# Second mixer of a two-layer decoder step: the first half of the output projection is written ahead of the delta stage, and the memory projections are handed over in steps between the delta heads

## The chip, the cores and the metric

The kernel runs on one core of a Trainium2 chip. The metric is the device time of one execution in microseconds (us), the median of three runs. The profile is one more execution, taken by the hardware profiler. TensorE (PE in the rows; PEld is its weight load), VectorE (DVE), ScalarE (ACT), GpSimd (POOL) and the DMA queue of SyncE (SP) each work through a queue of their own, and semaphores tie them together.

## What is computed

The reference runs a trunk of two layers over 512 prompt tokens and 8 x 8 sample tokens (576 columns in all, width 1024). Each layer is a feed-forward block, a token mixer, a cross attention over 256 memory tokens and a second feed-forward block. The change is in the mixer of the second layer. Cut to what matters:

```python
def odd_mixer(h, ...):
    p = h @ w_in                                  # one input projection for both groups
    # group C: retention, 4 heads -> y_c (512 columns)
    # group D: RWKV-7 delta rule, 8 heads of 64 -> y_d (512 columns)
    #   S_t = S_{t-1} diag(w_t) + (S_{t-1} a_t) b_t^T + v_t k_t^T ;  o_t = S_t r_t
    return concat([y_c, y_d]) @ w_out             # one output projection, 1024 x 1024

def mem_kv(mem, mem_g, w_kv):                     # needs nothing of x
    k, v = split(rmsnorm(mem, mem_g) @ w_kv, 2)   # 256 x 1024 @ 1024 x 2048
```

So the half of the output projection that reads y_c can run as soon as the retention heads are done, and the keys and values of the memory can be computed at any time before the cross attention of that layer.

## The kernel before

**Layout.** Activations lie transposed, 128 features on the partitions and the 576 tokens along the free side, in two halves of 288 tokens (`TH`). A dense product is made from three fp32r products (`wh` and `wl` are the high and low part of a weight; `mm3`, line 331): eight output chunks, each over k = 4 or 8 blocks of 128, times three, times two halves. One half of the output projection is thus 8 x 4 x 3 x 2 = 192 matmuls of 288 columns. Its weights come in four loads of 0.5 MB through `unit` (line 300 issues the load, 317 casts `wh` on ScalarE, 318 makes `wl` on VectorE), and `add_x` (1597) adds each chunk to the residual.

**Memory projections.** `wkv` (lines 1396 to 1435) is a generator. Its first two steps load the memory, transpose it (1405) and form high and low parts (1412, 1413) in four buffers of the tag `y`. Its eight further steps are one unit each: a load of 1 MB (300), two casts on ScalarE (307), two subtractions on VectorE (308), 48 matmuls of 256 columns (lines 1427, 1428, 1429 in equal number), two scaled copies (1431), and, at the start of the next step, a store (1435). All eight are 384 matmuls. `y` has six buffers; the four split retention outputs `ys` and the two prepared pairs of heads 2 and 3 hold all six until the first half of the output projection is done.

**Delta stage.** `delta(j)` handles two of the eight 64-wide heads at once, so there are four of them, j = 0 to 3, in two lanes (j % 2). Each has: score matmuls (1134), a block inverse that goes through DRAM and back (`blocks`, lines 1062 to 1076) with 15 steps of small VectorE work (1070, 1073), products that complete the inverse (`inverse`), the operands of the recurrence, and then the recurrence itself, eight chunks in order. A step of it is two matmuls on TensorE, two additions on VectorE (1193), two matmuls, and the state update on VectorE (1200). A tail handles the sample tokens. `decays(j)` prepares a head, `bonus(j)` and `delta_out(j)` finish it. Heads 2 and 3 use the slots of heads 0 and 1 again, so they begin when those are through. In program order: `delta(0)`, `delta(1)`, `decays(2)`, `decays(3)`, `bonus`, `delta_out(0)`, `delta_out(1)`, `delta(2)`, `delta(3)`, `delta_out(2)`, `delta_out(3)`, first half of the output projection, all of `wkv`, second half.

**Order.** The queues are not written out by hand here. A planner runs over the whole program before it goes to the chip and lays each engine's instructions in a fixed order: of those that its own simulated clock says are ready, the one written earlier in the program goes first, and a later one is pulled ahead where the engine would otherwise be free and a buffer is there. On the chip each queue is then worked through in that fixed order. So what stands last in the program text need not run last.

Of the kernel before, what the change touches and what calls it, by code (L numbers as in the profile page):

```python
# [140 lines left out]
class Net:  # L141
# [1131 lines left out]
    def odd_mixer(self, filler, nxt):  # L1273
        nc, a, o = self.nc, self.a, self.o
        self.tmp = 't'
        self.lane = 0
        self.norm_finish()
        xn = self.xn
        w_in, w_out = a['odd_w_in'][0], a['odd_w_out'][0]
        tabs = []  # L1280
        for n in range(2):
            self.lane = 1
            t = self.ct('g')
            nc.sync.dma_start(t, a['c_rope'][:, n * T:(n + 1) * T])
            nc.vector.tensor_mul(t, t, self.rstd)
            tabs.append(t)
        self.cosr, self.sinr = tabs
        col = lambda g, h: w_in[:, g * 512 + h * P:g * 512 + (h + 1) * P]
        ys = []
        raw, ds, yd = {}, {}, {}  # L1290
        self.slot = [{}, {}]

        def proj(h):
            uq, uk = self.unit(col(0, h), col(1, h))
            qk = self.pair()
            q = self.rope(self.mm3(uq, xn), qk[:, 0])
            k = self.rope(self.mm3(uk, xn), qk[:, 1])
            uv, ug = self.unit(col(2, h), col(3, h))
            vt = self.token_major(self.col_scale(self.mm3(uv, xn)), 'm')
            return q, k, vt, self.silu_twice(self.mm3(ug, xn))  # L1300

        def mix(h, q, k, vt, sg):
            ys.append(self.head_norm(self.retention(h, q, k, vt), self.vec('ret_gnorm', h), sg, True))

        def low_rank():
            self.sh = self.cp.tile([P, 126], F32, tag="edge", bufs=1, name="sh")
            self.lh = self.cp.tile([P, 8], F32, name="lh")
            nc.scalar.mul(self.lh[:, :4], self.vec('rwkv_w0', 0, 4), 0.5)
            nc.scalar.mul(self.lh[:, 4:], self.vec('rwkv_a0', 0, 4), 0.5)
            self.la = self.kp.tile([P, T], F32, tag="acc", bufs=1, name="la")  # L1310
            uw, = self.unit(w_in[:, 3584:3712])
            self.shift_mix(self.mm3(uw, xn), 12, self.la)
            nc.scalar.activation(self.la[:64], self.la[:64], AF.Tanh)

        def gate():
            ug, = self.unit(w_in[:, 3712:3840])
            self.sgd = self.shift_mix(self.mm3(ug, xn), 13, None)
            nc.scalar.activation(self.sgd, self.sgd, AF.Tanh, scale=0.5)
            nc.vector.tensor_scalar(self.sgd, self.sgd, 0.5, 0.5, ALU.mult, ALU.add)
            ps = self.psm()  # L1320
            nc.tensor.transpose(ps[:126, :P], self.sh, self.ident)
            sht = self.small(P, tag="tok", bufs=3)
            nc.scalar.copy(sht[:126], ps[:126, :P])
            nc.sync.dma_start(o['shift_p'][0, 0].rearrange("(c p) -> c p", p=P), sht[:14])
            nc.sync.dma_start(o['shift_s'][0].rearrange("b (c p) -> (b c) p", p=P), sht[14:126])

        def decay(j):
            self.slot[j] = {f't{i}': self.ct('t') for i in range(3)}
            self.slot[j].update({f'g{i}': self.ct('g') for i in range(2, 6)})
            ds[j] = self.decays(j, *raw[j])  # L1330
            self.slot[j].update(g0=raw[j][0], g1=raw[j][1])

        for h in range(2):
            self.lane = h
            mix(h, *proj(h))
        self.lane = 0
        low_rank()
        raw[0] = self.prep(0, w_in)
        decay(0)
        self.lane = 1  # L1340
        for h in (2, 3):
            mix(h, *proj(h))
        raw[1] = self.prep(1, w_in)
        self.lane = 0
        self.bonus(ds[0])
        self.lane = 1
        decay(1)
        self.lane = 0
        ys = [self.split(y) for y in ys]
        raw[2] = self.prep(2, w_in)  # L1350
        self.lane = 1
        self.bonus(ds[1])
        raw[3] = self.prep(3, w_in)
        self.lane = 0
        gate()
        for n in range(2):
            self.lane = n
            wide = [self.ct2(n) for _ in range(4)]
            self.slot[n].update({f'x{i}': wide[i // 2][:, i % 2] for i in range(8)})
            self.slot[n].update({f't{i}': self.ct('t') for i in range(3)})  # L1360
        for pair in ((0, 1), (2, 3)):
            for j in pair:
                self.lane = j % 2
                self.delta(j, ds[j])
            for j in pair if pair[0] == 0 else ():
                self.lane = j % 2
                ds[j + 2] = self.decays(j + 2, *raw[j + 2])
            for j in pair if pair[0] == 0 else ():
                self.lane = j % 2
                self.bonus(ds[j + 2])  # L1370
            for j in pair:
                self.lane = j % 2
                yd[j] = self.delta_out(j, ds[j])
        self.lane = 0
        self.out_proj(w_out[:512], ys, None)
        self.run(filler())
        self.out_proj(w_out[512:], [self.split(yd[j]) for j in range(4)], nxt)


# [510 lines left out]
```

## Time and profile before

| | |
|---|---|
| median of 3 runs | 2960.69 us (2960.6 to 2961.26) |
| profiled execution | 2950.59 us |
| its span, first to last instruction | 2948.8 us |
| mean granted TensorE clock | 0.979 |
| TensorE busy (its ends are modelled) | 2872.8 us, 97% |
| VectorE / ScalarE / GpSimd busy | 2100.4 / 1253.9 / 421.7 us |

[...] Rows below are stamped in us from the start of the span.

### The profile page before, as it was taken

To read this page: it belongs to the slowest core of one execution; us is meant where nothing else is said; L and a number is where in the kernel's file an instruction comes from. 1 tells how busy PE (TensorE), PEld (TensorE's weight loads), DVE (VectorE), ACT (ScalarE), POOL (GpSimd) and SP (SyncE) were. 2 spreads that over 40 slices of the span, in tenths; PEclk is the share of its full clock that TensorE was granted. 3 is DMA by queue.
4 is the path that set the end of the run, shared out by engine and by line. 5 is a ranking of instruction groups with operands and counts; after the bars stand their busy time and mean duration, and the time that the engine had idled before them with its cause. 6 is when DMAs were issued, how large, how long until landed. Compare 5 with 4: busy or idle time off the path is not lost.

```text
span 2948.8 us, 54661 instructions
## 1 busy us (share of the span) xinstructions
PE 2872.8 (97%) x22324; PEld 2718.9 (92%) x22324; DVE 2100.4 (71%) x3786; ACT 1253.9 (43%) x2257; POOL 421.7 (14%) x384
## 2 busy tenths in 40 slices
PE   8999999999999999999999999999989999999998
PEld 8999998999988999999999999888768787999998
DVE  7988866555546698886988875657577546698884
ACT  6544442222535544445444444343243434544443
POOL 1100012111100210002100111213222100210001
PEclk9999999999999999999999999999779999999999
DMA  4332222222445232222323232222112235232322
GB/s 139 102 99 90 87 83 59 87 74 94 143 172 176 76 104 86 90 87 76 97 91 98 89 95 78 75 76 64 38 44 83 91 138 196 74 103 87 100 76 65
DMA packets 343250, 278.76 MB, mean 95 GB/s; under 512 B 27332, under 2 KB 326168, under 8 KB 343000
## 3 DMA queue, kind: packets, MB, share of 16 engines
q1 hardware_dynamic: 343000, 275.27, 29.6%
q8 instruction: 176, 2.88, 0.4%
q14 instruction: 74, 0.61, 0.1%
HBM read 262.09 MB, written 13.14 MB: 93 GB/s over the span
## 4 chain that ended last, share of the span: by engine, by line
PE 86%; DVE 6%; ACT 3%; DMA 2%; issue 2%; POOL 1%; SPq 0%; ACTq 0%; POOLq 0%; DVEq 0%
PE pm L347 23%; PE pd L331 21%; PE pd L1768 18%; PE pd L347 4%; PE pd L1741 3%; PE pm L1741 2%; PE pm L1025 2%; PE pm L945 1%; DVE wf L1648 1%; PE pd L1459 1%; DMA S<-ffn_w_down 1%; PE pd L1428 1%; PE pm L509 1%; PE pd L1427 1%; PE pd L1429 1%
## 5 line engine op out<-in xcount | busy, mean ns | idle before, releaser
L347 PE MATMUL pm<-xf,wf 128*128 128x288 f32 x5472 | 763.7, 295 | 1.8 <-DVE g L566 1.6
L347 PEld LDWEIGHTS pm<-xf,wf 128*128 128x128 f32 x5472 | 740.6, 188 | 2.6 <-ACT wf L1647 1.8
L331 PE MATMUL pd<-x,wh 128*128 128x288 f32 x2368 | 430.8, 301 | 1.2 <-ACT t L894 1.2
L331 PEld LDWEIGHTS pd<-x,wh 128*128 128x128 f32 x2368 | 354.7, 191 | 6.5 <-ACT t L894 1.4
L1597 DVE SCALAR_TENSOR_TENSOR xT<-pd,xT 128x576 f32<-128x576 f32 x240 | 181.3, 756 | 249.0 <-PE pd L1768 185.5
L1768 PE MATMUL pd<-m,wf 128*128 128x288 f32 x2112 | 339.0, 296 | 5.5 <-DVE xT L1597 3.5
L1768 PE MATMUL pd<-g,wf 128*128 128x288 f32 x2112 | 337.9, 295 | 0.0
L560 POOL TENSOR_TENSOR g<-g,rstd 128x576 f32<-128x576 f32 x88 | 152.2, 1746 | 1271.9 <-DVE t L1680 561.9
L1768 PEld LDWEIGHTS pd<-m,wf 128*128 128x128 f32 x2112 | 301.1, 188 | 7.5 <-issue 4.4
L1768 PEld LDWEIGHTS pd<-g,wf 128*128 128x128 f32 x2112 | 299.3, 188 | 0.2
L1647 ACT CAST wf<-raw 128x512 fp32r<-128x512 f32 x276 | 168.2, 619 | 299.5 <-PE pd L1768 166.8
L331 PE MATMUL pd<-x,wl 128*128 128x288 f32 x1184 | 261.6, 301 | 0.0
L1648 DVE TENSOR_TENSOR wf<-raw,wf 128x512 fp32r<-128x512 f32 x276 | 216.2, 787 | 20.6 <-ACT wf L1647 20.6
L317 ACT CAST wh<-raw 128x1024 fp32r<-128x1024 f32 x106 | 111.1, 1048 | 281.7 <-PE pd L331 235.4
L1647 ACT CAST wf<-t 128x512 fp32r<-128x512 f32 x228 | 141.9, 622 | 187.4 <-PE pm L347 75.5
L331 PEld LDWEIGHTS pd<-x,wl 128*128 128x128 f32 x1184 | 193.3, 191 | 1.5
L1647 ACT CAST wf<-S 128x512 fp32r<-128x512 f32 (+1 forms) x192 | 112.5, 586 | 149.2 <-PE pm L347 72.1
L331 PE MATMUL pd<-y,wh 128*128 128x288 f32 x896 | 171.3, 308 | 0.3 <-DVE xT L1597 0.3
L1648 DVE TENSOR_TENSOR wf<-t,wf 128x512 fp32r<-128x512 f32 x228 | 157.3, 690 | 4.7 <-ACT wf L1647 4.7
L331 PEld LDWEIGHTS pd<-y,wh 128*128 128x128 f32 x896 | 136.7, 194 | 4.6 <-DVE xT L1597 0.6
L318 DVE TENSOR_TENSOR wl<-raw,wh 128x1024 fp32r<-128x1024 f32 x106 | 130.6, 1232 | 13.4 <-ACT wh L317 9.6
L1648 DVE TENSOR_TENSOR wf<-S,wf 128x512 fp32r<-128x512 f32 (+1 forms) x192 | 123.6, 644 | 20.2 <-ACT wf L1647 19.9
(522 smaller groups left out, 4805.4 us busy)
## 6 DMA issues: line engine op xcount, KB each, us to landing
raw<-ffn_w_gu SPq DMA_DIRECT2D x88, 1024.0 KB
S<-ffn_w_down SPq DMA_DIRECT2D x160, 256.0 KB
raw<-xattn_wkv SPq DMA_DIRECT2D x16, 1024.0 KB
x<-cache_mem_v SPq DMA_DIRECT2D x32, 512.0 KB
raw<-cache_mem_k SPq DMA_DIRECT2D x16, 1024.0 KB
raw<-odd_w_in SPq DMA_DIRECT2D x30, 512.0 KB
raw<-even_w_in SPq DMA_DIRECT2D x16, 512.0 KB
raw<-xattn_wq SPq DMA_DIRECT2D x8, 1024.0 KB
```

The lines of the kernel that those rows point to most:

```text
L317: nc.scalar.copy(h, raw[:, :, c:c + step])
L318: nc.vector.tensor_sub(l, raw[:, :, c:c + step], h.bitcast(F32))
L331: nc.tensor.matmul(ps[:, hf, :TH], w[:, k], x[:, hf * TH:(hf + 1) * TH], start=(k == 0 and w is wh and xi == 0), stop=(k == nk - 1 and w i ...
L347: self.nc.tensor.matmul(ps, a[:, j], b[:, j], start=(not more and j + i == 0), stop=(j == n - 1 and i == 2), skip_group_check=more)
L509: nc.tensor.matmul(ps[hf][:, :TH], lhsT, sq[:, hs])
L560: nc.gpsimd.tensor_mul(t, t, self.rstd)
L1025: self.nc.tensor.matmul(ps[q, c * 64:(c + 1) * 64], *fn(c, q))
L1597: self.nc.vector.scalar_tensor_tensor(x, ps, s, x, ALU.mult, ALU.add)
L1647: self.nc.scalar.copy(h, src)
L1648: self.nc.vector.tensor_sub(l, src, h.bitcast(F32))
L1741: self.nc.tensor.matmul(d['ps'][t][:, :TH], (wh, wh, wl)[i][:, j], xs[i == 1][:, j], start=(k + j + i == 0), stop=(k == 1 and j == 3 and i ...
L1768: nc.tensor.matmul(ps[:, hf, :TH], a[:, k], b[:, hf * TH:(hf + 1) * TH], start=(k + i == 0), stop=(k == nk - 1 and i == 2))
```

## The change

The first half of the output projection is written before the delta stage, the generator of the memory projections is made there and advanced by its two preparing steps, and it is advanced by two units after each `delta(j)`. What is left of it (the last store) runs at its old place.

```diff
         self.lane = 0
         gate()
+        self.out_proj(w_out[:512], ys, None)
+        mem = filler()
+        next(mem), next(mem)
         for n in range(2):
...
             for j in pair:
                 self.lane = j % 2
                 self.delta(j, ds[j])
+                self.lane = 0
+                next(mem), next(mem)
...
         self.lane = 0
-        self.out_proj(w_out[:512], ys, None)
-        self.run(filler())
+        self.run(mem)
         self.out_proj(w_out[512:], [self.split(yd[j]) for j in range(4)], nxt)
```

No instruction is added or taken away; only the place in the program is another, and with it the order in which the planner takes things up.

## Rows read from the trace of the kernel before

**Rows 1.** Page, part 2: granted TensorE clock in 40 slices of the span.

```profile
PEclk9999999999999999999999999999779999999999
```

**Rows 2.** Chain that ended last, 1990 to 2440: start us, us, what.

```profile
2006.22 19.20 PE pd L331 x144
...
2340.07 18.75 PE pd L331 x142
```

**Rows 3.** Busy time by stretch: us, then engines, PEclk, DMA share, GB/s.

```profile
2031.00:2057.00 26.00, 24.15 (x329) 19.70 (x329) 18.26 (x62) 13.10 (x36) 6.83 (x11) 1.00 0.28 80
...
2088.00:2118.00 30.00, 30.00 (x224) 23.14 (x224) 12.23 (x37) 1.50 (x2) 1.75 (x2) 0.51 0.04 6
...
2137.00:2160.00 23.00, 21.10 (x195) 15.58 (x195) 17.20 (x44) 7.75 (x10) 5.78 (x8) 0.85 0.04 8
2160.00:2185.00 25.00, 22.48 (x105) 13.62 (x104) 14.01 (x28) 11.70 (x21) 4.95 (x7) 0.66 0.19 54
2185.00:2216.00 31.00, 27.41 (x286) 22.31 (x286) 27.41 (x54) 21.31 (x41) 9.71 (x13) 0.89 0.22 59
2216.00:2244.00 28.00, 27.57 (x438) 23.70 (x434) 23.56 (x72) 11.63 (x28) 5.20 (x8) 1.00 0.39 106
2244.00:2272.00 28.00, 27.56 (x364) 22.61 (x361) 21.31 (x57) 7.71 (x14) 5.05 (x6) 1.00 0.22 63
...
2288.00:2312.00 24.00, 22.59 (x220) 17.53 (x220) 14.67 (x41) 8.73 (x12) 0.00 (x0) 1.00 0.12 38
```

**Rows 4.** The same stretches, matmuls of line 331 alone: PE, PEld.

```profile
2006.00:2031.00 25.00, 25.00 (x188) 24.95 (x189) 1.00 0.31 96
2031.00:2057.00 26.00, 5.89 (x32) 4.26 (x32) 1.00 0.28 80
...
2088.00:2118.00 30.00, 13.07 (x39) 9.11 (x37) 0.51 0.04 6
```

**Rows 5.** The same for line 1427, a third of the memory projections.

```profile
2216.00:2244.00 28.00, 7.07 (x24) 4.54 (x24) 1.00 0.39 106
```

**Rows 6.** VectorE in order of time: state updates of the recurrences, first and last.

```profile
2086.63 0.27 DVE L1200 SCALAR_TENSOR_TENSOR x<-pm,s,t 128x64 f32<-128x64 f32 x1
...
2116.70 0.28 DVE L1200 SCALAR_TENSOR_TENSOR x<-pm,s,s 128x64 f32<-128x64 f32 x1 [0.55 <-PE pm L1025]
...
2136.76 0.28 DVE L1200 SCALAR_TENSOR_TENSOR x<-pm,s,t 128x64 f32<-128x64 f32 x1 [0.42 <-PE pm L1025]
...
2138.89 0.28 DVE L1200 SCALAR_TENSOR_TENSOR x<-pm,s,s 128x64 f32<-128x64 f32 x1 [0.67 <-PE pm L1025]
...
2159.11 0.28 DVE L1200 SCALAR_TENSOR_TENSOR x<-pm,s,s 128x64 f32<-128x64 f32 x1 [0.39 <-PE pm L1025]
...
2249.12 0.28 DVE L1200 SCALAR_TENSOR_TENSOR x<-pm,s,t 128x64 f32<-128x64 f32 x1
...
2271.43 0.28 DVE L1200 SCALAR_TENSOR_TENSOR x<-pm,s,s 128x64 f32<-128x64 f32 x1
...
2288.05 0.28 DVE L1200 SCALAR_TENSOR_TENSOR x<-pm,s,t 128x64 f32<-128x64 f32 x1 [2.35 <-PE pm L1025]
...
2311.67 0.28 DVE L1200 SCALAR_TENSOR_TENSOR x<-pm,s,s 128x64 f32<-128x64 f32 x1 [0.72 <-PE pm L1025]
```

**Rows 7.** SyncE's DMA queue in order of time: loads of the output projection.

```profile
2012.87 8.60 SPq L300 DMA_DIRECT2D raw<-odd_w_out  x3
...
2032.36 0.56 SPq L300 DMA_DIRECT2D raw<-odd_w_out  x1
```

**Rows 8.** TensorE in order of time: first transposes of the memory.

```profile
2146.96 0.76 PE L1405 MATMUL pd<-cblob,raw 128*128 128x128 f32 x5
```

**Rows 9.** Single lines (ns min/median/max, first and last start): memory projections, their weights' low parts.

```profile
L1427 PE MATMUL pd<-wh,y x256: 274/283/582, 707.2 to 2328.5; 128*128 128x256 f32 x128
...
L308 DVE TENSOR_TENSOR wl<-raw,wh x32: 1210/1225/1889, 688.5 to 2311.9; 128x1024 fp32r<-128x1024 f32 x32
```

**Rows 10.** Waits of SyncE's queue, 2025 to 2335: us in total, times, longest.

```profile
SPq L300 <- DVE x L1200: 31.9, 3, 18.4
```

## The prediction, made before the changed kernel was run

> **What bounds the kernel now.** I read the page first. TensorE is busy for 97% of the span, and its granted clock is full everywhere but in two of 40 slices [rows 1]; these cover 2064 to 2211 us, the delta stage of the second mixer. Outside that stage dense products run back to back: 188 matmuls of line 331 in 25 us, 133 ns each [rows 4]. There only less work on TensorE would help, and the change takes none away. So I looked at the delta stage alone.
>
> The chain in order of time shows its borders: a dense run of line 331 that begins at 2006 and another one from 2340, the second half of the output projection and what follows it [rows 2]. From 2031 on line 331 is down to 32 matmuls in 26 us [rows 4]: the heads have begun. What lies between, some 300 us, is what the change can move. The table of busy time by stretch says what limits it. In the two first recurrences and behind them the clock is 0.51, 0.85 and 0.66, in the second pair of heads it is 1.00 [rows 3]. TensorE's weight loads fill 13.6 of 25 us in the stretch from 2160, and VectorE is at 27.4 of 31 us from 2185 and 23.6 of 28 from 2216. So the stage is a chain of short steps between TensorE and VectorE, with independent matmuls laid into its gaps, and neither engine is at its limit throughout.
>
> What lies in the gaps already is the point to see. The first half of the output projection stands behind all four heads in the program, yet 32 of its matmuls run before 2057 and 39 more in the first recurrence [rows 4]. The memory's first transposes start at 2147 [rows 8], as that half ends and its `y` buffers come free. The units of the memory projections then run through the second pair of heads: 24 matmuls on each of three lines from 2216 to 2244 [rows 5]. The change therefore does not give an idle engine work. It changes which filler runs where: the output projection ahead of the first scores in one block, the memory projections in the first pair of heads, and little or nothing in the second.
>
> **The change part by part.**
>
> *The projection in front.* Its four loads, four casts, four subtractions, 192 matmuls and eight residual additions move ahead of `delta(0)`. Three of the loads are issued at 2013 to 2021 already, the fourth at 2032 [rows 7], so the weights are there. 192 x 133 ns = 25.5 us dense; 32 of them (4.3 us) run in that stretch anyway. The heads start 21.2 us later. Bounds: 0, if the planner still lets the scores go first, and 25.5. I take 21.2, since TensorE and its weight loads are already filled in 2031 to 2057 (24.2 and 19.7 of 26 us) by the heads' own matmuls, which now wait.
>
> *What that buys in the first pair.* The first recurrence takes 30.1 us for seven steps (2086.63 to 2116.70, 4.30 each) at a clock of 0.51. The second takes 22.4 us (3.19) at 0.85 with filler in it, the third 22.3 (3.19) at 1.00 with memory units in it [rows 3, 6]. In the changed kernel memory units lie where the output projection lay, as in the third. If the clock holds, 30.1 becomes 22.4: -7.7. Bounds: 0 and -7.7; I take -7.7.
>
> *What it buys in the second pair.* The memory units start when the projection's buffers are free, near 2060 in place of 2147, and there are eight. In the old kernel they took from 2147 to 2328 [rows 8, 9], some 23 us each, in the lowest rank. At that pace they would end near 2241, and in their new rank earlier, so the third and fourth recurrence are nearly bare. The shortest step beside little filler is 2.13 us (2136.76 to 2138.89 [rows 6]); at that rate seven steps take 14.9 us, against 22.3 and 23.6 (2288.05 to 2311.67): -16.1 at best, 0 at worst. I take -10, over half, since the fourth head's inverse still shares the third recurrence.
>
> *VectorE in front of the second pair.* A subtraction for a memory unit takes 1.22 us [rows 9]. Seven of the 16 lie between 2185 and 2244 (two for each 16 matmuls of line 1427), on an engine that is 84 to 88% busy there [rows 3]. Gone: -8.6 at best, 0 at worst; I take -6. They move into the first pair, where VectorE is at 12.2 of 30 us in the first recurrence, and take the place of the projection's own casts and additions; so nothing is charged there. With that cover gone, 8.6 us come back.
>
> *Behind the first pair.* [...] TensorE has few matmuls there (105 in 25 us from 2160). Two memory units now rank ahead of `decays(2)`, and may keep it busy. [...]
>
> *Queues and rank.* The nine loads of 1 MB pass the DRAM round trip of `blocks` on SyncE's queue earlier than before. A load that waits for its buffer holds that queue: three of them waited 31.9 us in sum [rows 10]. Most of it is idle queue; a round trip caught behind one pays what is left of the wait, 0 to some 5 us; I take 0. Two units (96 matmuls, by columns 118 ns each, 11 us) now rank ahead of `delta(1)` and two ahead of `decays(2)`; they stand in for 160 matmuls of the projection (21 us) that lay there. I take 0, bounds +-5.
>
> Sum: 21.2 - 7.7 - 10 - 6 - 5 = -7.5 us.
>
> *The clock, weighed.* The row: the first recurrence, with 39 large matmuls spread over 30 us, ran at 0.51, and the fourth, with a unit and a half laid in, at 1.00 [rows 3, 4]. [...]
>
> **Rivals.**
> 1. *The forecast*, -7.5, within -2 to -16.
> 2. *The order does not matter.* Filler costs the same wherever it lies: 21.2 in front is given back by 7.7 in the first pair, 10 in the second and 3 on VectorE, and the clock behind the first pair stays as it is: +0.5, 2961.2 us. For it: the last memory unit starts at 2328 [rows 9], just before the dense run, so filler and heads ended together before too; against it: a block ahead of the scores delays them in full, while filler in gaps delays in part.
> 3. *Slower: the second pair runs cold.* Bare, it has only short matmuls, and the clock falls as in the first recurrence. There a step took 4.30 us with 39/7 large matmuls of about 0.27 us in it; bare that is some 2.8, little below 3.2, so its 10 us are not gained, nor VectorE's 6 or the 5 behind the first pair. And 2216 to 2244, with weight loads in 23.7 of 28 us, stretches; I put 4 on it. 21.2 - 7.7 + 4 = +17.5, 2978.2 us. It decides once the mean clock from 2216 on is under about 0.8. [...]
> 4. *More gain.* The clock holds throughout and the late recurrences are truly bare: 21.2 - 7.7 - 16.1 - 8.6 - 12 = -23.2, 2937.5 us.
>
> That the change does nothing, the planner drawing the same order, I hold to be out: the projection was ready at 2031 and lay behind the scores only by its place in the program.
>
> **How the numbers follow.** Forecast 0.38, the second 0.20, the third 0.33, the fourth 0.09. The profiled execution took 2950.59 us, its span 2948.8; a change of the span moves both alike, so the forecast there is 2943.1. The median of the timed runs stands 10.1 us higher at 2960.69; with -7.5 it becomes 2953.2. What this kernel's timing can tell from no change is about 0.2%, 5.9 us. Of the forecast 0.05 lies within that: faster 0.33 + 0.09 = 0.42, same 0.20 + 0.05 = 0.25, slower 0.33. The range runs from 2934, below the fourth case, to 2982, above the third by some of its unknowns; the likeliest case alone would be 2945 to 2959.
>
> **What would show it.** Right: line 331 runs dense from 2031 to about 2057 and the first state update comes near 2108 in place of 2087; the first transposes of the memory near 2060; the last unit before the fourth head's recurrence; third and fourth recurrences of 15 to 19 us; the clock at 1.00 in the first recurrence. Wrong: a first state update near 2087 (the front is free, and the gain larger), or a clock near 0.5 in the second pair (third case), or memory units that still end beside the last tail (second case).

## The result and the profile after

The changed kernel takes 2983.05 us (median of four runs, 2977.01 to 2991.56) against 2960.64 us for the kernel before beside it: a ratio of 1.0108 with an interval of 1.0079 to 1.0137, slower by some 22 us. Timed again, beside 13 runs of the kernel before, it took 2979.15 against 2950.25 us, 1.0100 [1.0073, 1.0126]. The forecast of 2953.2 us was wrong in sign, and the result lies just above the range. It is nearest the third case (2978.2 us, the second pair runs cold).

The profiled execution is the slowest of the four, 2991.56 us, span 2989.8 us, mean granted clock 0.968 (a share of the full clock, 1.00). It stands 41.0 us above the profiled execution of before; how the 22 and the 41 go together is told with the last experiments, under "Time against the clock".

First the page's row of the granted clock in 40 slices of the new span, to be read against [rows 1].

```profile
PEclk9999999999999999999999999999887699999999
```

There are four slices below 9 in place of two. By stretch (start:end, us, then busy time and count for PE, PEld, DVE, ACT and POOL, granted clock, DMA share, GB/s), as in [rows 3]:

```profile
2033.00:2061.00 28.00, 26.21 (x197) 25.97 (x197) 12.94 (x17) 5.15 (x6) 2.51 (x3) 1.00 0.41 120
...
2117.00:2146.00 29.00, 28.89 (x243) 22.76 (x245) 12.24 (x37) 1.75 (x3) 1.75 (x2) 0.59 0.16 42
2165.00:2188.00 23.00, 22.56 (x215) 17.71 (x215) 17.37 (x39) 10.69 (x13) 5.27 (x5) 1.00 0.19 59
...
2213.00:2244.00 31.00, 21.58 (x105) 14.86 (x105) 25.52 (x41) 14.08 (x27) 11.64 (x12) 0.63 0.21 63
2244.00:2284.00 40.00, 31.43 (x578) 26.72 (x577) 30.54 (x101) 15.27 (x41) 8.88 (x14) 0.91 0.24 62
2284.00:2305.00 21.00, 20.44 (x218) 16.22 (x216) 11.10 (x35) 0.16 (x1) 2.42 (x3) 0.50 0.04 5
2305.00:2327.00 22.00, 14.82 (x206) 10.77 (x205) 7.21 (x15) 9.44 (x18) 6.92 (x8) 0.81 0.08 15
2327.00:2351.00 24.00, 23.30 (x167) 16.27 (x165) 10.90 (x36) 0.81 (x2) 0.00 (x0) 0.50 0.00 1
2351.00:2376.00 25.00, 14.75 (x70) 7.79 (x71) 7.47 (x15) 7.16 (x11) 3.12 (x3) 0.57 0.07 12
```

The first line is the moved half of the projection, dense. From 2216 to 2376 the mean clock is 0.68. The third and the fourth recurrence (2284 to 2305 and 2327 to 2351) run at 0.50, the lowest value in any row of the two traces; before, the whole second pair ran at 1.00. The same view for line 331 alone:

```profile
2006.00:2033.00 27.00, 25.56 (x191) 25.53 (x192) 1.00 0.35 106
2033.00:2061.00 28.00, 26.13 (x195) 25.82 (x194) 1.00 0.41 120
2117.00:2146.00 29.00, 0.00 (x0) 0.00 (x0) 0.59 0.16 42
```

And three single lines of the trace that answer to [rows 8, 9] (nanoseconds min/median/max, first and last start; 1409 and 1431 are the old 1405 and 1427):

```profile
L1409 PE MATMUL pd<-cblob,raw x32: 271/273/332, 697.0 to 2062.8; 128*128 128x128 f32 x32
L1431 PE MATMUL pd<-wh,y x256: 274/283/828, 705.3 to 2239.4; 128*128 128x256 f32 x128
L308 DVE TENSOR_TENSOR wl<-raw,wh x32: 1175/1225/2437, 686.3 to 2220.0; 128x1024 fp32r<-128x1024 f32 x32
```

Two rows of TensorE in order of time show what else came ahead of the scores: a transpose that stood 1.79 us behind GpSimd, and the memory's last 16 transposes.

```profile
2036.25 0.33 PE L1321 MATMUL pm<-cblob,sh 128*126 128x128 f32 x1 [1.79 <-POOL sh L938]
...
2060.93 2.11 PE L1409 MATMUL pd<-cblob,raw 128*128 128x128 f32 x16
```

The last memory matmul starts at 2239.4 in place of 2328.5: all eight units lie ahead of the second pair, which is bare (but for 12 matmuls of line 331, the second half, that reach into the fourth recurrence). The state updates of the recurrences, first and last of the first, third and fourth, on VectorE in order of time, against [rows 6]:

```profile
2116.78 0.27 DVE L1200 SCALAR_TENSOR_TENSOR x<-pm,s,t 128x64 f32<-128x64 f32 x1
2146.29 0.28 DVE L1200 SCALAR_TENSOR_TENSOR x<-pm,s,s 128x64 f32<-128x64 f32 x1 [0.36 <-PE pm L1025]
...
2284.31 0.28 DVE L1200 SCALAR_TENSOR_TENSOR x<-pm,s,t 128x64 f32<-128x64 f32 x1 [3.09 <-PE pm L1025]
2304.86 0.28 DVE L1200 SCALAR_TENSOR_TENSOR x<-pm,s,s 128x64 f32<-128x64 f32 x1 [0.28 <-PE pm L1025]
...
2327.09 0.28 DVE L1200 SCALAR_TENSOR_TENSOR x<-pm,s,t 128x64 f32<-128x64 f32 x1
2350.66 0.28 DVE L1200 SCALAR_TENSOR_TENSOR x<-pm,s,s 128x64 f32<-128x64 f32 x1 [1.16 <-PE pm L1025]
```

Bare, the third recurrence takes 20.55 us (22.3 before) and the fourth 23.57 (23.6 before). The chain puts the dense second half, which stood at 2340.07 in [rows 2], here:

```profile
2036.58 17.85 PE pd L331 x134
...
2375.61 22.18 PE pd L331 x154
```

The ledger below cuts each trace at the same five points: the first score matmul (line 1134), the first and last state updates of each recurrence, the first of head 3's two output products on VectorE (1270; added lines move these numbers a little in some kernels) and the end of the span. All is in us, worked out from the start times of these instructions. "Between the pairs" runs from the last state update of the second recurrence to the first of the third.

| kernel | first score at | to end of 2nd recurrence | between the pairs | 3rd | between | 4th | to head 3's output | rest | span |
|---|---|---|---|---|---|---|---|---|---|
| before | 2031.7 | 127.4 | 90.0 | 22.3 | 16.6 | 23.6 | 24.4 | 612.7 | 2948.8 |
| changed | 2063.0 | 125.3 | 96.1 | 20.6 | 22.2 | 23.6 | 23.4 | 615.8 | 2989.8 |
| changed, a2 | 2058.7 | 115.6 | 96.1 | 20.5 | 22.2 | 23.6 | 23.3 | 618.8 | 2978.9 |
| e1 | 2062.9 | 110.5 | 102.4 | 18.6 | 16.2 | 23.0 | 25.0 | 617.0 | 2975.5 |
| e3 | 2058.3 | 115.6 | 92.4 | 19.6 | 15.6 | 20.8 | 22.5 | 617.5 | 2962.2 |
| e4 | 2065.3 | 112.1 | 84.1 | 20.1 | 19.0 | 20.5 | 21.5 | 614.0 | 2956.6 |
| g1 | 2031.3 | 155.7 | 81.3 | 20.5 | 22.2 | 20.2 | 22.3 | 614.8 | 2968.3 |
| h1 | 2030.0 | 112.8 | 88.8 | 19.7 | 18.5 | 21.1 | 23.3 | 661.7 | 2975.8 |

From the first row to the second: +31.3 in front (1.6 of it is this run's later start of the dense run that precedes, 2007.82 against 2006.22), -2.1 in the first pair, +8.8 from there to head 3's output, +3.0 behind: 41.0.

### The profile page after: what moved, and what is told of

Read it like the earlier page. It is cut to its first block, busy times and chain, and to the rows that moved or that the text cites. A ratio compares the mean times of both kernels' runs of the same rounds, so it can differ in the third digit from the quotient of the medians.

```text
span 2989.8 us, 54666 instructions
## 1 busy us (share of the span) xinstructions
PE 2884.0 (96%) x22324; PEld 2729.4 (91%) x22324; DVE 2102.8 (70%) x3786; ACT 1253.8 (42%) x2257; POOL 424.6 (14%) x384
## 4 chain that ended last, share of the span: by engine, by line
PE 85%; DVE 6%; ACT 3%; DMA 2%; issue 2%; POOL 1%; SPq 0%; ACTq 0%; POOLq 0%; DVEq 0%
PE pm L347 23%; PE pd L331 20%; PE pd L1772 17%; PE pd L347 4%; PE pd L1745 3%; PE pm L1025 2%; PE pm L1745 2%; PE pm L509 1%; PE pd L1433 1%; PE pd L1431 1%; PE pd L1463 1%; PE pd L1432 1%; DMA S<-ffn_w_down 1%; PE pm L945 1%; PE pm L1556 1%
## 5 line engine op out<-in xcount | busy, mean ns | idle before, releaser
L1652 DVE TENSOR_TENSOR wf<-raw,wf 128x512 fp32r<-128x512 f32 x276 | 216.4, 788 | 20.6 <-ACT wf L1651 20.6
L331 PE MATMUL pd<-y,wh 128*128 128x288 f32 x896 | 163.9, 302 | 2.2 <-ACT y L437 2.2
L1652 DVE TENSOR_TENSOR wf<-S,wf 128x512 fp32r<-128x512 f32 (+1 forms) x192 | 123.7, 644 | 21.5 <-ACT wf L1651 21.4
```

The source lines that it names most:

```text
L331: nc.tensor.matmul(ps[:, hf, :TH], w[:, k], x[:, hf * TH:(hf + 1) * TH], start=(k == 0 and w is wh and xi == 0), stop=(k == nk - 1 and w i ...
L1652: self.nc.vector.tensor_sub(l, src, h.bitcast(F32))
```

## The experiments

Theory A puts the loss on the block ahead of the scores, theory B on the second pair, which is bare and cold (at 0.50, as in the rows above). In the first expectation below, "theory C" is the units' new rank; from i1 on the same letter stands for another theory, told there. The first four expectations give times beside a kernel before of 2960.7 us. It took 2949.49 us beside these runs, so they are read here as ratios of 2960.7: 2965 us, for example, as 1.0015.

**The projection in front alone (e1).** The generator stays at its old place, lowest in rank.

```diff
         gate()
+        self.out_proj(w_out[:512], ys, None)
...
-        self.out_proj(w_out[:512], ys, None)
         self.run(filler())
```

> Only the projection is ahead of the heads; the memory projections stand at their old place, behind all heads, in the lowest rank. Theory A (the block in front): its 25.5 us and the wait it makes are the whole loss, so the time is that of the changed kernel, 2983 +- 6 us, whatever the second pair's clock. Theory B (the second pair runs bare and cold): the units still start near 2062 us, when the buffers come free, and run out before the second pair, so 2977 to 2985 as well, with a clock near 0.5 there. Theory C (the units' new rank ahead of head 1 and of the next decays is what costs): 2965 to 2972.

2975.33 us against 2949.49, 1.0079 [1.0060, 1.0098]. By ratio that lies within theory A (1.0055 to 1.0096) and theory B (1.0055 to 1.0082), which this run doesn't tell apart, and outside theory C (1.0015 to 1.0038). The units are gone early all the same: the last memory matmul starts at 2231.0, since the planner takes up whatever is ready as soon as an engine is free. The clock of the third and fourth recurrence is 0.68 and 0.62. Over three quarters of the loss come with the block and with what the planner then does; what the rank of the units adds (1.0079 against 1.0100) isn't clear of the noise. The opposite (steps between the heads, projection at its old place) wasn't tried, for the units need the `y` buffers that only the projection frees.

**Extra filler in the lowest rank (e3).** The change, with 192 added matmuls of 288 columns on data that is there, ahead of the last store; one column of each result is copied to a small tile that nobody reads.

```diff
+        t = self.pair(F32R)
+        nc.scalar.copy(t, self.xT[:, :2])
+        for _ in range(8):
+            ps = self.psd()
+            for n in range(24):
+                nc.tensor.matmul(ps[:, n % 2, :TH], t[:, 0, :P], t[:, 1, n % 2 * TH:(n % 2 + 1) * TH])
+            nc.vector.tensor_copy(self.small(1, tag="wm"), ps[:, 0, :1])
         self.run(mem)
```

> The changed kernel with 192 more matmuls of 288 columns, whose results nobody reads, in the lowest rank but for the last store, free to run when the memory projections are through: 25.5 us more for TensorE, laid into the second pair of heads. Theory A: no gain, 2983 to 3000 us. Theory B: the clock of the second pair rises towards 1.00, its recurrences and the tail shorten, and the time falls to 2965 to 2977 us in spite of the added work.

2972.12 us, 1.0076 [1.0047, 1.0105]: 25.5 us more of TensorE's dense work, and the kernel is not slower than the change (1.0100 [1.0073, 1.0126]); that its median is lower isn't clear of the noise. By ratio it stands at the lower edge of theory A (1.0075 to 1.0133) and above theory B (1.0015 to 1.0055), while the trace shows what B foretold: the clock rose and the second pair became shorter. The matmuls all fell between 2200 and 2311. The third recurrence, the time between it and the fourth, and the fourth, in the same view as above:

```profile
2266.00:2286.00 20.00, 20.00 (x264) 15.74 (x264) 13.75 (x38) 0.22 (x2) 2.51 (x3) 1.00 0.05 6
2286.00:2301.00 15.00, 14.85 (x211) 10.45 (x207) 4.59 (x11) 5.24 (x12) 6.11 (x8) 1.00 0.12 22
2301.00:2322.00 21.00, 19.37 (x194) 14.27 (x193) 12.40 (x38) 5.11 (x8) 0.82 (x1) 1.00 0.00 1
```

The clock is back at 1.00. Up to the end of the second recurrence e3 and a2 agree to 0.5 us (ledger); from there to head 3's output e3 is 14.9 us shorter: 3.7 between the pairs, 6.6 between the recurrences, 3.8 in the two recurrences, 0.8 in the tail. This is what the filler gave the second pair and the stretch ahead of it in these two profiles, and most of it lies outside the recurrences. Not all of it need be the clock: with the added matmuls the planner also laid VectorE's instructions of this stretch in another order in some 30 places.

**Four units held back (e4), and all eight (e5).** In e4 the last four units are held on TensorE's queue: one behind the first scores of head 2, one behind its operands, and the same with head 3. In e5, which leaves out `u > 3`, all eight are held so, two to each head.

```diff
         scores(tb, Aab, Arb)
+        self.marks.append(self.last_pe())
...
+        self.marks.append(self.last_pe())
         Z, o = S('x0'), S('x7')
...
                     nc.tensor.matmul(ps[:, m, :256], mh[:, ms], wh, start=(k == 0), stop=False)
+                    if l and u > 3 and k == 0:
+                        self.behind(self.marks[u])
```

> The changed kernel with the last four units of the memory projections held on TensorE's queue behind head 2's scores, head 2's operands, head 3's scores and head 3's operands. Same work. Theory A: the block in front is still paid, 2978 to 2986 us. Theory B: the second pair keeps its clock, 2960 to 2970 us; the rest above 2960.7 is what the block costs.

2956.07 us, 1.0025 [1.0009, 1.0042], within theory B by ratio (0.9998 to 1.0031): three quarters of the loss are gone with no work added or removed. Its third and fourth recurrence, now with a unit each:

```profile
2261.00:2282.00 21.00, 21.00 (x268) 17.00 (x268) 12.71 (x36) 3.72 (x7) 3.32 (x3) 1.00 0.17 46
2301.00:2321.00 20.00, 20.00 (x203) 15.23 (x197) 11.78 (x33) 9.00 (x12) 0.50 (x1) 1.00 0.37 120
```

They take 20.1 and 20.5 us, no more than the bare ones of the change at 0.50, and the stretch between the pairs shrinks from 96.1 to 84.1, more than the second pair gains. Not every stretch is warm here either: the second recurrence, now bare, has 0.56.

> As the last, with all eight units held, one behind each head's scores and one behind each head's operands. Theory A: 2978 to 2986 us. Theory B: 2960 to 2970 us, and less than with four held if the stretch behind the first pair is warmed too.

2975.04 us, 1.0083 [1.0062, 1.0105]: a miss for theory B, and by ratio within theory A (1.0058 to 1.0085). The second pair is warm (1.00 in both recurrences, some 20 and 21 us). With two units held behind each head the stretch behind the first pair ran dry instead: its clock was 0.50 from 2200 to 2220, and it took 98.4 us. It was not enough to have filler in the second pair.

**The change again (a2), and the block placed elsewhere (f3, g1).** f3 is e4 with the projection ahead of `gate()`, g1 (behind the mark of left-out lines; their old place is left out) is e4 with the projection and the two preparing steps behind `delta(0)`.

```diff
-        gate()
         self.out_proj(w_out[:512], ys, None)
+        gate()
...
                 self.delta(j, ds[j])
+                if j == 0:
+                    self.out_proj(w_out[:512], ys, None)
+                    next(mem), next(mem)
                 next(mem), next(mem)
```

> The changed kernel itself, beside the others on one chip, so that they can be set against it. Both theories: 1.008 to 1.013 of the kernel before.

2979.15 us, 1.0100 [1.0073, 1.0126], as given above.

> The kernel with four units held for the second pair, and the projection written ahead of gate() too: the 1.8 us for which TensorE stood behind the transpose of the shift rows now lie under the heads' start or under dense work. Theory A and B alike: 1 to 4 us less than with four units held, 0.999 to 1.002 of the kernel before.

2968.28 us, 1.0066 [1.0042, 1.0090]: a miss. The first scores come at 2058.5. The first pair is short (100.5 us), but the clock falls behind it, 0.73 on average over the 99 us between the pairs, and the third recurrence, with 48 matmuls of the units in it, takes 27.4 us at 0.68 where e4's took 20.1 at 1.00 with as many.

> Four units held for the second pair, and the projection with the memory's preparation written behind delta(0) in place of ahead of it. Theory A (the block ahead of the scores): head 0 starts near 2031 us again, and up to 25 us come back against the kernel with four units held: 0.992 to 0.998 of the kernel before. Theory B alone (the block costs nothing by its place, only the clock counts): as with four units held, 1.0009 to 1.0042.

2973.33 us, 1.0079 [1.0052, 1.0106]: a second miss, of theory A and of B alone. The first scores are back at 2031.3, and the second recurrence ends at 2187.0 all the same, for the block then stands between the first and the second (63.9 us from one to the other; 20.1 before), and the second, bare and at 0.50, takes 26.2 us. In both places tried the block, in one piece, costs its length or more.

**The old order with a bare second pair (h1).** All eight units wait for the last head's output; nothing else is changed.

```diff
+        self.end = self.last_pe()
         self.out_proj(w_out[:512], ys, None)
         self.run(filler())
...
                     nc.tensor.matmul(ps[:, m, :256], mh[:, ms], wh, start=(k == 0), stop=False)
+                    if l and k == 0:
+                        self.behind(self.end)
```

> The kernel before with all eight units of the memory projections held behind the last head's output, so that the second pair has no filler at all and the units' 384 matmuls run dense behind it, some 45 us. If a bare pair is shorter, as the prediction had it (16 to 25 us saved), 20 to 31 us slower than before (1.007 to 1.010). Theory B (bare means cold, nothing saved): 40 to 50 us slower (1.013 to 1.017), with a clock near 0.5 in the second pair.

2989.11 us, 1.0138 [1.0108, 1.0167]. From the end of the second recurrence to head 3's output it takes 171.3 us against 176.9 with eight units in the gaps: taking 384 matmuls out saves 5.6 us (some 5 of it in the two recurrences), with a clock that falls to 0.57 and 0.53, and behind the pair they cost 49.0 (rest, 661.7 against 612.7). The prediction counted on 16 us from emptying the pair (10 in the recurrences, 6 on VectorE). The time fits theory B. Three stretches of h1, its first, third and fourth recurrence:

```profile
2083.00:2103.00 20.00, 19.56 (x241) 15.32 (x242) 13.23 (x44) 1.57 (x2) 1.75 (x2) 1.00 0.06 9
...
2231.00:2252.00 21.00, 19.91 (x226) 15.88 (x226) 12.53 (x37) 1.08 (x4) 2.79 (x3) 0.57 0.05 8
2270.00:2291.00 21.00, 18.32 (x152) 12.50 (x148) 11.93 (x38) 2.36 (x3) 0.00 (x0) 0.53 0.00 1
```

The first line is a find. This recurrence has the order of the kernel before and the same 40 projection matmuls in it:

```profile
2085.00:2105.00 20.00, 8.56 (x40) 5.79 (x41) 1.00 0.05 9
```

It takes 18.8 us (state updates at 2083.11 and 2101.95); in the profile of before it took 30.1 at 0.51 [rows 3, 4, 6]. The change's own two profiles differ in the same way: one order, 29.5 us at 0.59 in the one and 20.0 at 1.00 in a2, whose row is

```profile
2112.00:2133.00 21.00, 20.45 (x256) 15.94 (x253) 13.95 (x42) 1.85 (x4) 1.75 (x2) 1.00 0.20 50
```

So the clock of that stretch is not settled by the order; it differs from execution to execution.

**Matmuls added inside the recurrences (i1 to i3).** Theory C, the second of that name: a recurrence is as long as its chain of short steps. 45 matmuls of 128 columns in each treated recurrence, three behind each product of a step: in i1 in the first two of the old order, in i2 in the last two of the change, in i3 in all four. (j2's trace, below, has two records for each fp32 product of this size, 192 for 96.)

```diff
                     nc.vector.tensor_add(u, u, pu[q])
+                if j in (2, 3):
+                    self.warm(wu, bt, 3)
...
             nc.vector.scalar_tensor_tensor(nxt, pz, e, zk, ALU.mult, ALU.add)
+            if j in (2, 3):
+                self.warm(wz, bt, 3)
```

> The old order, with 45 matmuls of 128 columns added to each of the first two recurrences (three behind each product of a step), whose results nobody reads. Theory B (the clock is what a recurrence costs): the old first recurrence took 30.1 us at 0.51 and the second 22.4 at 0.85; with the added matmuls both show 0.9 to 1.00 and take 19 to 22 us, and the first pair ends 5 to 12 us earlier, a ratio of 0.996 to 0.999. Theory C (a recurrence is as long as its chain of short steps, whatever the clock, and added matmuls stand in its way): the first pair ends 0 to 10 us later, 1.000 to 1.004.

> The change, with 45 matmuls of 128 columns added to each of the third and fourth recurrences. Theory B: the two recurrences go from 20.6 and 23.6 us at about 0.5 to 16 to 20 us at 0.9 to 1.00, and with the products behind them the pair ends 6 to 12 us earlier; the ratio falls from 1.010 to 1.006 to 1.008. If the cold is paid outside the recurrences (products, inverse, tail), the ratio stays at 1.009 to 1.011; if the added matmuls only stand in the way, 1.012 to 1.015.

> The change, with 45 matmuls of 128 columns added to each of the four recurrences. Theory B: as with the third and fourth alone, 1.005 to 1.008, and the stretch behind the first pair at 0.9 or more. Theory C: twice what the third and fourth alone cost above the change, 1.013 to 1.018.

1.0064 [1.0043, 1.0084], 1.0136 [1.0103, 1.0168] and 1.0168 [1.0137, 1.0199]: i1 lies above both of its ranges, i2 and i3 where the added matmuls stand in the way. The clock came, in i1 1.00 in both treated recurrences (in i2 0.81 and 1.00):

```profile
2087.00:2119.00 32.00, 31.99 (x380) 26.94 (x381) 14.57 (x46) 0.59 (x1) 3.00 (x5) 1.00 0.04 6
2132.00:2168.00 36.00, 35.55 (x289) 27.54 (x286) 22.34 (x53) 8.86 (x14) 6.07 (x8) 1.00 0.12 36
```

The time did not: 31.7 and 35.9 us, and in i2 34.7 and 30.3. Theory C holds for matmuls that stand between the steps: they are paid. The full clock came without that price only from work that yields to the chain, the lowest rank of e3 and the units of e4. (i1 lost in an untreated place too: its fourth recurrence took 30.4 us at 0.72, 23.6 at 1.00 before.)

**The same between the pairs (j1 to j3).** 96 matmuls of 128 columns, four behind each product of `halves` in the preparation of heads 2 and 3, their bonus and the outputs of heads 0 and 1; in the old order, in the change and in e4.

```diff
             self.nc.tensor.matmul(ps[:, :TH], lhsT, rhs[:, hf * TH:(hf + 1) * TH])
+            for _ in range(4 if self.hot else 0):
+                self.nc.tensor.matmul(ps[:, 384:], self.ident, self.ident)
```

> The old order, with 96 matmuls of 128 columns added between the pairs, four behind each product of the preparation of heads 2 and 3, of their bonus and of the outputs of heads 0 and 1; nobody reads them. In the old kernel the stretch from the last state update of the second recurrence to the first of the third took 90.0 us at clocks from 0.66 to 1.00. If the clock is what it waits for, the stretch takes 82 to 86 us at 0.9 to 1.00 and the ratio is 0.996 to 0.999, a version that beats both kernels. If VectorE and ScalarE set its pace, it takes 89 to 93 us and the ratio is 1.000 to 1.004.

> The change with the same 96 matmuls. There the stretch took 96 us. If the clock is what it waits for, it takes 86 to 91 us and the ratio falls from 1.010 to 1.006 to 1.008; if the memory units crowd it, it stays at 94 to 98 us with the clock at 0.9 or more, and the ratio at 1.009 to 1.013.

> The change with its last four units held back for the second pair, and the same 96 matmuls. Held back alone, the stretch took 84 us and the ratio was 1.0025. If the clock still costs there, 78 to 82 us and 1.000 to 1.002; if only the crowding had cost, 83 to 87 us and 1.002 to 1.006.

1.0115 [1.0074, 1.0156], 1.0119 [1.0090, 1.0149] and 1.0095 [1.0063, 1.0127]: j1 and j3 above all their ranges, j2 in its second one by ratio. The stretch took 104.7, 101.9 and 104.4 us, and in j2 it had a clock of 1.00 throughout. But the readers of these products waited for the added matmuls. In j2, by engine, tile and line, the time that they made others wait (us, times):

```profile
  ACT g L988: 9.7, 4
  DVE t L968: 2.2, 4
  DVE y L1020: 1.1, 2
  DVE x L1265: 0.9, 1
```

Of these 13.9 us, 6.9 lie ahead of the stretch, in the second recurrence, where the first of these products already run. The 7.0 us inside it, taken off 101.9, leave 94.9, some 1 below the 96.1 of the change. That is an estimate (not all of these waits need lie on the chain), and by it a full clock alone gives little there.

What the units do in this stretch, a third of them each (line 1427 of before and its like in the change, e3 and h1), from the last update of the second recurrence to the first of the third:

```profile
2159.11:2249.12 90.01, 17.24 (x57) 11.07 (x57) 0.86 0.27 73
2188.25:2284.31 96.06, 10.28 (x32) 6.45 (x32) 0.84 0.22 58
2173.87:2266.24 92.37, 10.09 (x32) 6.89 (x32) 0.96 0.22 61
2142.79:2231.57 88.78, 0.00 (x0) 0.00 (x0) 0.78 0.13 30
```

The change has fewer matmuls of the units there than the kernel before, not more, and the old order without any (h1) takes 88.8 us. So the units alone don't make the stretch long. How much of the 12 us that e4 gained in it is the clock and how much the order in which the planner takes up the work there, no run settles.

**Time against the clock.** All timed executions carry a mean granted clock. 58 of the kernel before, beside the experiments (the four of the first comparison aren't among them), go from 0.986 (2934.75 us) to 0.973 (2962.82 us). A straight line through them falls by 2.30 us for each 0.001 of clock, and they lie 1.8 us around it. The six executions of a2 have a median clock of 0.972; by that line the kernel before would take 2965.9 us there. So of the 29 us of that comparison (2979.15 - 2950.25) some 13 are left at the same clock and some 16 go with the lost clock. For e4 (0.9805) the line gives 2946.3, and 9.8 are left. It is a line of one order laid beside others, so an estimate; for kernels with added matmuls it says little, since those buy clock with work (e3: clock 0.9825, 30 above the line). The profiles differ by 41 us and the medians by 22 because the profiled execution of before lies 10 us below its median, and that of the change 8.5 above its own, with the lowest clock of its four (0.968); in both profiles the first recurrence was cold (0.51 and 0.59).

## Why the prediction was wrong

Set against the ledger of the two profiles, the forecast misses by 48.5 us (+41.0 in place of -7.5). 17.1 of them lie between the pairs, 8.5 in front, 8.2 in the third and fourth recurrence, 5.6 in the first pair, and 5.6 between the third recurrence and the fourth (22.2 us at 0.81 in place of 16.6 at 1.00; e3, at 1.00, took 15.6), which no term of the forecast spoke of; the rest is 3.6.

- **The projection in front, +21.2: under-sized.** The scores came 29.7 us later (31.3 less the run's 1.6). The dense stretch of line 331 takes 26.1 us in its row, near the 25.5 of the sum; the 2.1 us of the memory's transposes came ahead of the scores too, and 1.8 us in which TensorE stood behind GpSimd. The credit of 4.3 us was an error: the 32 projection matmuls of 2031 to 2057 lay beside the heads' own, and taking them out there gave nothing back up to the first score.
- **First recurrence, -7.7: not the change's to gain.** Mechanism as foretold in a2 (20.0 us at 1.00), but the old order does that too (18.8 at 1.00 in h1), and both orders have it cold in other executions. Taken cold with cold, the first pair took 127.4 and 125.3 us, and warm with warm 112.8 and 115.6. One profiled stretch at 0.51 was read as a property of the order.
- **Second pair bare, -10: the step whose mechanism failed.** The forecast took the clock of the old pair, 1.00, to hold in the bare one; it was 0.50. The two recurrences gave 1.8 us, for the fourth took as long as before. 14.9 us, seven times the shortest step, was reached by none; the shortest anywhere, f3's first two, took 16.5 us at 1.00 (18 matmuls of the units in it) and 17.2 at 0.87 (none). With memory units at 1.00 the third and fourth take 20.1 and 20.5 (e4), bare at about 0.5 to 0.6 they take 19.7 to 23.6 (h1, the change): what emptying them may save, the lower clock takes back in good part (an estimate from these times). A third and fourth recurrence bare at full clock were not measured.
- **VectorE, -6, and the clock behind the first pair, -5: neither came, and this is the largest miss.** The stretch that both terms speak of took 96.1 us in place of 90.0. Three of the seven subtractions stayed in it, VectorE's busy time is 69.1 us in it against 70.5, and the clock is 0.84 against 0.86. The first output of head 0 (line 1270) came at 2228.10 in place of 2183.94, 39.9 us behind the second recurrence instead of 24.8. Why the stretch grew is not shown. That the units crowded it is not borne out: in e5 none of their matmuls lies ahead of that output, and it comes 45.4 us behind the second recurrence. e3, with as many of them as the change and the clock at 0.96, takes 92.4, though its order differs too. What is left may lie in the order in which the planner took up the preparation of heads 2 and 3 and the outputs; no run isolates it. That a fuller clock behind the first pair saves the 5 us of the forecast, or the 12 of its fourth case, no run shows: j2 had 1.00 throughout this stretch and comes, less the waits for the added matmuls, to an estimated 94.9 us against the change's 96.1.
- **The clock, weighed.** The forecast took the 1.00 of the second pair's rows for a property of the chain; with the units taken out it fell to 0.57 and 0.53 (h1) and to 0.50 (the change), and with some put back it was 1.00 (e4). So the trace agrees with the third case: 0.50 in both recurrences of the second pair. What is laid into a stretch doesn't tell the clock of every one: in the first recurrence before, the rows have TensorE busy for all of 30.0 us at 0.51 [rows 3], and the same order had 1.00 in h1.
- **The third case** had the right mechanism and the right point (0.68 from 2216 to 2376, and it was to decide under 0.8). Its sum, +17.5, charged 4 us for the cold, where e3 and a2 differ by 14.9 (clock and order together); and it kept the -7.7 of the first pair. That it comes within 5 us of the measured median is in part luck: its front is 8.5 us short and that gain was not the change's.
- **Queues, taken at 0.** SyncE's queue shows up in no step of the ledger as a cost; no run tested it by itself.

The loss is thus not one thing: by the line above, an estimate, about half of the 29 us of the second comparison is the order at like clock (a block of 25.5 us taken out of gaps, less what the gaps give back) and about half is lost clock, itself an outcome of the new order, and in a2's profile the clock is 1.00 from 2000 to 2190: what the delta stage lost of it lies behind the first pair (0.84 from 2174 to 2270, 0.50 in the third and fourth recurrence). No version here beats the kernel before; e4 comes nearest, at 1.0025.

## What to carry to other kernels

Work that lies in the gaps of a latency-bound chain (one whose steps wait for each other) can cost a fraction of its length: 384 matmuls cost a net 5.6 us here, the clock that they held included, against 49.0 behind the chain. So it is not saved by being moved to a dense block, and a chain that is emptied gains little where the clock falls with it (the 5.6 us of h1, at 0.57 and 0.53). Before filler is spent early, ask which later stretch it lies in at full clock (here the second pair: 1.00 with units in it, 0.50 to 0.57 without), and try sharing it out over the thin stretches, in a rank that yields to the chain (e4, 1.0025 against the change's 1.0100). And one profile is one execution: the clock of a single stretch may be read as a property of the kernel only if a second execution of the same order shows it.

## What the runs showed of the hardware

- The same instructions in the same order ran a recurrence at 1.00 in one execution and at 0.51 to 0.59 in another (18.8 against 30.1 us, and 20.0 against 29.5). What decided it, no run here shows; of the change, the 25 us and more ahead of it were at 1.00 in both.
- A recurrence filled with large matmuls pays for the low clock (the first: 30.1 us at 0.51, 18.8 at 1.00, one order; the third with 48 in it: 27.4 at 0.68 in f3, 20.1 at 1.00 in e4). One without large matmuls pays too, how much varies with the order: the second took 17.2 at 0.87 in f3, 19.8 at 0.56 in e4 and 26.2 at 0.50 in g1.
- Over 58 executions of one kernel, 0.001 of mean clock went with 2.30 us, 0.078% of the time: four fifths of the 0.1% that it would be, by an estimate from the median clock of 0.979, if every step of the kernel went with TensorE's clock.
- 192 matmuls of 288 columns, added in the lowest rank, did not lengthen the kernel they were added to (1.0076 against 1.0100), while 90 and 180 matmuls of 128 columns between the steps brought the change to 1.0136 and 1.0168 (i2, i3), and 90 and 96 in the path brought the old order to 1.0064 and 1.0115 (i1, j1). The 96 of j2 (1.0119) lie within the change's own interval.
